# RWKV mixer steps laid on other ticks between the matmuls of a hybrid SSD and RWKV-7 block

## The chip, the cores and the metric

The kernel runs on one core of a Trainium2 chip. The metric is the device time of one execution in microseconds (us). Before the change it is 1671.96 us, the median of three runs (1670.29 to 1674.27). The engines are TensorE (PE, with its weight loads PEld), VectorE (DVE), ScalarE (ACT), GpSimd (POOL) and SyncE (SP), which issues the DMAs.

## What is computed

One block of a streaming encoder on x of 256 frames by 2048 channels: a norm, one input projection, two mixers (a Mamba-2 SSD and an RWKV-7), one output projection, and a SwiGLU FFN. The change touches the RWKV-7 mixer alone. Its core in the reference:

```
def step(S, inp):
    r_t, w_t, k_t, v_t, a_t, b_t = inp
    sa = jnp.einsum('bhvk,bhk->bhv', S, a_t)
    S = S * w_t[:, :, None, :] + sa[..., None] * b_t[:, :, None, :] + v_t[..., None] * k_t[:, :, None, :]
    return S, jnp.einsum('bhvk,bhk->bhv', S, r_t)
...
y = wkv7_scan(rh, decay.reshape(b, s, H, N), kh, vh, -kk, kk * ah)
mu = jnp.mean(y, axis=-1, keepdims=True)
var = jnp.mean(jnp.square(y - mu), axis=-1, keepdims=True)
y = ((y - mu) * lax.rsqrt(var + GN_EPS)).reshape(b, s, D_RWKV) * gn_w.astype(f32) + gn_b.astype(f32)
bonus = jnp.sum(rh * kh * r_k.astype(f32).reshape(H, N), axis=-1, keepdims=True) * vh
y = y + bonus.reshape(b, s, D_RWKV)
return y * g
```

The kernel does the scan in four chunks of 64 frames, for 32 heads, four heads (256 channels, a "pair" of channel blocks) at a time: eight pairs, 0 to 7.

## The kernel before

**Main matmuls.** Every projection is done as three fp32r matmuls (high by high, low by high, high by low). A weight unit of 512 KB is loaded by SP into `raw` (4 buffers), rounded by ACT into `whi` (L192), and the rest is subtracted by DVE into `wlo` (L193), four buffers each, so ACT and DVE can run up to four units ahead of PE. `gemm_a` (L277 to L279) takes four units of 24 matmuls for 256 columns; `gemm_b` (L305 to L307) takes units of 12 matmuls and adds its result into h (L318).

**Stretches.** The RWKV part runs over the pairs. The stretch of pair pi holds the three `gemm_a` of its k, v and r (12 units) and, from pair 4 on, behind v, two column groups of the output projection of finished pairs (4 units). So the stretches of pairs 0 to 3 are short (12 units) and those of pairs 4 to 7 long (16 units). A `gemm_a` advances a clock of ticks by four, a column group by two: 12 and 16 ticks. Two more windows follow, behind the last pair, of 20 and 18 ticks.

**Side work.** `window(pi, ticks)` lays the steps of three pairs on these ticks, in the class `Side`, a heap that is emptied as the clock passes: preparation of pair pi (table `PREP`), matrices of pair pi-1 (`AMATS`) and the inverse of its chunk matrices (`INV`), and the chain over the chunks of pair pi-2 (`CHAIN`). In short stretches, `INV` and `CHAIN` are multiplied by 11.5/16. What is not placed when a stretch ends is emitted there by `drain`. A step is a group of instructions of several engines; a scheduler then makes each engine's order out of the emitted program and the tiles' buffers. Each engine works through its order strictly.

**The steps that matter here.**

- `recept` and `sums` (L541 to L567): `sums` multiplies r by k on DVE, sums per head (`red`, L539), adds the halves on PE (`ps_sum`, L557) and makes `nn` and `bon`.
- `amat` and `across`: products of ar with bt and kt on PE (`ps_a`, L602 and L619), masked by DVE into `atb` and `atk` (L605, L622).
- `inv_out` sends the 16x16 blocks of `atb` out by eight DMAs and reads them back as rows (`nb`); `inv_rows`, `inv_level(4)` and `inv_level(8)` invert them on DVE (`pd`, L685, `tt` and `xb`, L687), doubling from 4x4 to 8x8 and to 16x16 blocks; `inv_in` takes `xb` out and back (`sc_X`, `cm`) and makes `X` on DVE (L701); `lev16a`, `lev16b`, `lev32a` and `lev32b` double on to 64 on PE (`ps_b`, L712) with DVE or ACT steps between (`t1s`, `XT`, `XF`).
- For each chunk c of 0 to 3: `step_r` (`ps_r`, L766, copied by ACT to `rs`), `step_w` (`ps_w`, L780, scaled by DVE to `ws`), `step_s` (the state `ps_s`, L796 and L799, made `sn` by DVE, L804 to L807; and the result `ps_y`, L814, copied by ACT to `Y`).
- `gnorm`: mean on DVE, eight squares on ACT (`ysq`, L833), a table load and a square root (L834), reciprocal and product on DVE, eight scalings on ACT (L838). `gnorm2` and `final` apply the weights, the bonus and the gate, and hand over yh and yl for the output projection. `vt`, `btt`, `ktt` and `yc` are transposes whose quarters ACT copies (L581).

The 8 PSUM banks stand in two pools of four: one for the main matmuls, one for all the side steps.

Of the kernel before, what the change touches and what calls it, by code (L numbers as in the profile page):

```python
# [16 lines left out]
P = 128  # L17
# [14 lines left out]


PREP = (1.081, 1.2, 4.2, 5.2, 5.536, 6.756, 8.05, 9.2)
AMATS = (0.132, 1.4, 2.027, 2.231, 2.69, 3.323, 6.493)
INV = (4.9, 5.9, 6.9, 8.4, 10.4, 11.4, 12.9, 14.9)
STEPS = (0.667, 2.0, 5.0)
SSD = (0.9, 2.7, 4.842, 6.642, 8.442, 8.924, 10.724, 12.524, 12.657, 16.124)
CHAIN = (0.05, 0.6, 1.4, 2.4, 3.4, 4.0, 4.9, 5.9, 6.5, 7.4, 8.4, 9.0, 9.9, 11.4, 12.9, 13.4)


class Side:
# [26 lines left out]
def tile_hybrid_block(ctx: ExitStack, tc: tile.TileContext, x, norm1_g, w_in, conv_w, conv_b, dt_bias, A_log, D_skip,  # L69
# [16 lines left out]
    side = Side()  # L86
# [4 lines left out]
    def mxt(name):  # L91
        return mx.tile([P, 512], F32, name=name, tag="mx")

    def bc(ap, n):
        return ap.unsqueeze(ap.ndim).broadcast_to(list(ap.shape) + [n])
# [346 lines left out]
    NCH = 8  # L442

    def rwkv_pair(pi, st):
        cb0 = 2 * pi

        def tl(name, shape=(P, 2, T), bufs=1, tag=None):
            return rp.tile(list(shape), F32, name=name, tag=tag or name, bufs=bufs)

        def pl(name, shape=(P, 2, T), bufs=1):  # L450
            return pp.tile(list(shape), F32, name=name, tag=name, bufs=bufs)

        def col(c, base, j):
            return c[:, base + cb0 + j:base + cb0 + j + 1]

        def ch(t):
            return t.rearrange("p b (c t) -> p (b c) t", c=4)
# [78 lines left out]
        def headsum(dst, src):  # L536
            tr = pl("tmp2", (P, NCH, 64))
            nc.vector.transpose(tr.rearrange("p c t -> p (c t)"), src.rearrange("p b t -> p (b t)"))
            nc.vector.tensor_reduce(dst.rearrange("p c s -> p (c s)"),  # L539
                                    tr.rearrange("p c (s t) -> p (c s) t", t=32), axis=AX.X, op=ALU.add)  # L540
# [7 lines left out]
        def sums():  # L548
            red, r, kp = st["red"], st["r"], st["kp"]
            rk = pl("tmp")  # L550
            for j in range(2):
                nc.vector.scalar_tensor_tensor(rk[:, j], r[:, j], col(colA, RK, j), kp[:, j], ALU.mult, ALU.mult)
            headsum(red[:, 1], rk)
            ps = mxt("ps_sum")
            po = ps[:, :16].rearrange("p (a c) -> p a c", a=2)
            for s in range(2):
                nc.tensor.matmul(po, sel[:, s], red[:, :, :, s], start=s == 0, stop=s == 1)  # L557

            nn = tl("nn", (P, NCH + 4), 3)
            nc.vector.tensor_scalar(nn[:, :NCH], po[:, 0], 1e-24, -2.0, ALU.max, ALU.mult)  # L560
            nc.vector.reciprocal(nn[:, :NCH], nn[:, :NCH])
            for hh in range(2):
                nc.scalar.copy(hd(nn, 1 - hh)[:, NCH:], hd(nn, hh)[:, 4:NCH])
            bon = tl("bon", (P, NCH), 3)
            nc.vector.tensor_copy(bon, po[:, 1])
            st["nn"], st["bon"] = nn, bon

        def hd(t, hh):
            return t[hh * 64:(hh + 1) * 64]
# [20 lines left out]
        def amat(name, key, half):  # L590
            def f():
                if half == 0:
                    st[name] = tl(name, (P, NCH, 2, 64), 2)
                dst = st[name]
                src = ch(st[key])
                if name == "atb" and half == 1:
                    across(dst, src)
                    return
                ps = mxt("ps_a").rearrange("p (c t) -> p c t", c=4)
                for c in range(4):  # L600
                    for hh in range(2):
                        nc.tensor.matmul(hd(ps, hh)[:, c], hd(src, hh)[:, half * 4 + c],  # L602
                                         hd(st["ar"], hh)[:, half * 4 + c].rearrange("p a t -> p (a t)"),
                                         start=True, stop=True)
                nc.vector.tensor_tensor(dst[:, half * 4:half * 4 + 4].rearrange("p c a t -> p c (a t)"), ps,  # L605
                                        mask2.rearrange("p a t -> p (a t)").unsqueeze(1).broadcast_to([P, 4, P]),
                                        ALU.mult)
                if name == "atb":
                    d = dst[:, 0:4, 0]
                    nc.vector.tensor_tensor(d, d, bc(st["nn"][:, 0:4], 64), ALU.mult)  # L610
            return f

        def across(dst, src):

            pa = [mxt("ps_a")[:, :256].rearrange("p (c t) -> p c t", c=4) for _ in range(2)]
            for c in range(4):
                for a in range(2):
                    for hh in range(2):
                        nc.tensor.matmul(hd(pa[a], hh if a else 1 - hh)[:, c], hd(src, hh)[:, 4 + c],  # L619
                                         hd(st["ar"], hh)[:, 4 + c, a], start=True, stop=True)  # L620
            for a in range(2):
                nc.vector.tensor_tensor(dst[:, 4:8, a], pa[a], mask2[:, a].unsqueeze(1).broadcast_to([P, 4, 64]),  # L622
                                        ALU.mult)
            d = dst[:, 4:8, 0]
            nc.vector.tensor_tensor(d, d, bc(st["nn"][:, NCH:NCH + 4], 64), ALU.mult)
# [148 lines left out]
        def step_w(c):  # L774
            def f():
                rs = st["rs"]
                pw = [mxt("ps_w")[:, :64] for _ in range(2)]
                for hh in range(2):
                    for j in range(2):
                        nc.tensor.matmul(hd(pw[j], 1 - hh if j else hh), hd(st["XF"], hh)[:, 4 * j + c],  # L780
                                         hd(rs, hh)[:, j], start=True, stop=True)
                ws = tl("ws", (P, 2, 64), 2)
                for j in range(2):
                    nc.vector.tensor_scalar(ws[:, j], pw[j], st["nn"][:, 4 * j + c:4 * j + c + 1], None, ALU.mult)
                st["ws"] = ws
            return f
# [37 lines left out]

        def gnorm():
            Y = st["Y"]
            mv = tl("mv", (P, 2, NCH), 2)
            nm, rs = mv[:, 0], mv[:, 1]
            nc.vector.tensor_reduce(nm, Y, axis=AX.X, op=ALU.add)
            nc.vector.tensor_scalar(nm, nm, -1.0 / 64, None, ALU.mult)  # L830
            sq = tl("ysq", (P, NCH, 64))
            for c in range(NCH):
                nc.scalar.activation(sq[:, c], Y[:, c], AF.Square, bias=nm[:, c:c + 1], accum_out=rs[:, c:c + 1])  # L833
            nc.scalar.activation(rs, rs, AF.Sqrt, bias=epsg, scale=1.0 / 64)  # L834
            nc.vector.reciprocal(rs, rs)
            nc.vector.tensor_tensor(nm, nm, rs, ALU.mult)
            for c in range(NCH):
                nc.scalar.activation(Y[:, c], Y[:, c], AF.Identity, bias=nm[:, c:c + 1], scale=rs[:, c:c + 1])  # L838

# [14 lines left out]
        def final():  # L854
# [3 lines left out]
            for j in range(2):  # L858
                for kk in range(2):
# [7 lines left out]
            nc.scalar.copy(yh, yo)  # L867
            nc.vector.tensor_tensor(yl, yo, yh.bitcast(F32), ALU.subtract)

        amats = [recept, sums, amat("atb", "bt", 0), amat("atb", "bt", 1), inv_out, amat("atk", "kt", 0),  # L870
                 amat("atk", "kt", 1)]
        inv = [inv_rows, inv_level(4), inv_level(8), inv_in, lev16a, lev16b, lev32a, lev32b]
        chain = [load2]
        for c in range(4):
            chain += [step_r(c), step_w(c), step_s(c)]
        chain += [gnorm, gnorm2, final]
        return dict(load=load, decay=decay, rate=rate, keys=keys, keys2=keys2, keysum=keysum, vt=tok("vt", "v"),
                    btt=tok("btt", "bt"), ktt=tok("ktt", "kt"), amats=amats, inv=inv, chain=chain)

    pairs = []  # L880

    def window(pi, ticks):
        if pi < 8:
            w = pairs[pi]
            w["load"]()
            for t, n in zip(PREP, ("decay", "rate", "keys", "keys2", "keysum", "btt", "vt", "ktt")):
                side.at(t, w[n])
        if 0 < pi < 9:
            w = pairs[pi - 1]
            for t, f in zip(AMATS, w["amats"]):  # L890
                side.at(t, f)
            for t, f in zip(INV, w["inv"]):
                side.at(t if ticks >= 16 else t * (ticks - 0.5) / 16, f)
        if pi > 1:
            for t, f in zip(CHAIN, pairs[pi - 2]["chain"]):
                side.at(t if ticks >= 16 else t * (ticks - 0.5) / 16, f)

    held = []

# [8 lines left out]
    for pi in range(8):  # L908
        st = {}
        pairs.append(rwkv_pair(pi, st))  # L910
        window(pi, 16 if pi > 3 else 12)
        for i, (n, c) in enumerate((("k", CK), ("v", CV), ("r", CR))):
            ps = scaled(gemm_a(w_in, [(0, 256, c + pi * 256)], "ps_rkv"))
            t = pp.tile([P, 2, T], F32, name="rkv", tag="t" + n, bufs=1)
# [139 lines left out]
    for g in range(4):  # L1054
# [5 lines left out]
        for i in range(2):  # L1060
            ps = scaled(gemm_a(w_in, [(0, 256, CXBC + g * 512 + i * 256)], "ps_xs"))
            t = xz.tile([P, 2, T], F32, name="xc", tag=f"xc{i}")
# [98 lines left out]
    for b in range(2):  # L1161
        r = finish(2, b)
        for n in (2, 3, 0, 1):
            c = slice(n * 512, (n + 1) * 512)
            t = hg[b][n]
# [33 lines left out]
```

## Time and profile before

| What | Value |
|---|---|
| median of 3 runs | 1671.96 us (1670.29 to 1674.27) |
| profiled execution | 1671.13 us, of it the span 1669.4 us |
| mean granted clock of PE | 0.996 |
| PE busy | 1640.1 us, 98% of the span |
| DVE busy | 1172.9 us, 70% |
| ACT busy | 910.7 us, 55% |
| DMA read from HBM | 281.75 MB |

The span is the profiled part of the execution; 1.7 us lie around it. "Busy" is the time in which the engine had at least one instruction under way. A wait of an engine is put down to the instruction that released it. "Granted clock" is the clock that the throttle allows PE, 1 being full. The RWKV stretches lie between 38 and 512 us, the SSD part behind them up to 930 us, the FFN from there to the end.

### The profile page before, as it was taken

How to read it: one execution, taken by the hardware profiler on the slowest of the kernel's cores; microseconds unless marked ns; L12 is line 12 of the kernel's file. 1: busy time of each engine (PE TensorE's matmuls, PEld its weight loads, DVE VectorE, ACT ScalarE, POOL GpSimd, SP SyncE). 2: the span in 40 equal slices, each digit the busy share in tenths (PEclk: the TensorE clock that was granted, in tenths of full speed). 3: DMA queues.
4: the chain of work that ended last, by engine and by line, in shares of the span. 5: the costliest groups of instructions: out<-in, count | busy, mean ns of one | idle time of the engine just before them, and what ended most of it. 6: DMA issues, size and time to landing. Idle time of an engine off the chain costs nothing.

```text
span 1669.4 us, 31147 instructions
## 1 busy us (share of the span) xinstructions
PE 1640.1 (98%) x12514; PEld 1422.7 (85%) x12514; DVE 1172.9 (70%) x1827; ACT 910.7 (55%) x1488; POOL 17.9 (1%) x57
## 2 busy tenths in 40 slices
PE   8999999999999999999999999999999999999997
PEld 8998898988888988998988888888888888888886
DVE  7887898788887867877778656465565564554657
ACT  6654775766755648657665544444444444444444
POOL 3000000000000000000000000000000000000000
PEclk9998999999999999999999999999999999999999
DMA  8653554454455556765655666666666666666663
GB/s 247 184 143 104 134 135 126 137 140 139 138 142 144 154 152 188 233 191 155 180 176 152 202 189 190 194 189 189 196 190 189 190 189 196 189 191 192 190 189 126
DMA packets 219473, 286.97 MB, mean 172 GB/s; under 512 B 41762, under 2 KB 124480, under 8 KB 218688
## 3 DMA queue, kind: packets, MB, share of 16 engines
q1 hardware_dynamic: 218000, 282.68, 58.1%
q8 instruction: 98, 1.61, 0.4%
q0 software_dynamic: 752, 1.24, 0.3%
q10 hardware_dynamic: 576, 1.05, 0.2%
q14 instruction: 47, 0.39, 0.1%
HBM read 281.75 MB, written 3.18 MB: 171 GB/s over the span
## 4 chain that ended last, share of the span: by engine, by line
PE 77%; DVE 9%; ACT 6%; issue 3%; DMA 3%; SPq 1%; DVEq 0%; POOL 0%; ACTq 0%
PE ps_o L305 8%; PE ps_o L306 8%; PE ps_o L307 8%; PE ps_gt L306 5%; PE ps_up L307 5%; PE ps_gt L305 5%; PE ps_up L306 5%; PE ps_gt L307 5%; PE ps_up L305 5%; DVE wlo L193 2%; PE ps_xs L277 2%; ACT whi L192 2%; PE ps_rkv L277 2%; PE ps_xs L278 2%; PE ps_xs L279 2%
## 5 line engine op out<-in xcount | busy, mean ns | idle before, releaser
L193 DVE TENSOR_TENSOR wlo<-raw,whi 128x1024 fp32r<-128x1024 f32 x508 | 619.9, 1222 | 376.9 <-ACT whi L192 375.8
L192 ACT CAST whi<-raw 128x1024 fp32r<-128x1024 f32 x508 | 532.7, 1051 | 596.8 <-PE ps_o L307 159.6
L277 PE MATMUL ps_rkv<-uh,whi 128*128 128x256 f32 x768 | 227.7, 296 | 0.0
L279 PE MATMUL ps_rkv<-uh,wlo 128*128 128x256 f32 x768 | 218.9, 285 | 0.0
L278 PE MATMUL ps_rkv<-ul,whi 128*128 128x256 f32 x768 | 218.8, 285 | 0.0
L277 PEld LDWEIGHTS ps_rkv<-uh,whi 128*128 128x128 f32 x768 | 147.5, 192 | 5.3 <-issue 0.7
L278 PEld LDWEIGHTS ps_rkv<-ul,whi 128*128 128x128 f32 x768 | 147.9, 193 | 1.2 <-issue 0.3
L279 PEld LDWEIGHTS ps_rkv<-uh,wlo 128*128 128x128 f32 x768 | 147.6, 192 | 0.4
L305 PE MATMUL ps_gt<-whi,uh 128*128 128x512 f32 x352 | 137.1, 389 | 0.0
L307 PE MATMUL ps_gt<-whi,ul 128*128 128x512 f32 x352 | 137.0, 389 | 0.0
L306 PE MATMUL ps_gt<-wlo,uh 128*128 128x512 f32 x352 | 136.9, 389 | 0.0
L305 PE MATMUL ps_up<-whi,uh 128*128 128x512 f32 x352 | 136.9, 389 | 0.0
L306 PE MATMUL ps_up<-wlo,uh 128*128 128x512 f32 x352 | 136.9, 389 | 0.0
L307 PE MATMUL ps_up<-whi,ul 128*128 128x512 f32 x352 | 136.9, 389 | 0.0
L305 PE MATMUL ps_o<-whi,ah 128*128 128x512 f32 x336 | 131.7, 392 | 0.0
L307 PE MATMUL ps_o<-whi,al 128*128 128x512 f32 x336 | 130.9, 390 | 0.0
L306 PE MATMUL ps_o<-wlo,ah 128*128 128x512 f32 x336 | 130.7, 389 | 0.0
L305 PE MATMUL ps_o<-whi,yh 128*128 128x512 f32 x256 | 105.6, 412 | 0.0
L307 PE MATMUL ps_o<-whi,yl 128*128 128x512 f32 x256 | 100.9, 394 | 0.0
L306 PE MATMUL ps_o<-wlo,yh 128*128 128x512 f32 x256 | 100.8, 394 | 0.0
L318 DVE TENSOR_TENSOR h<-ps_o,h 128x512 f32<-128x512 f32 x152 | 98.5, 682 | 1.7 <-PE ps_o L307 1.1
L306 PEld LDWEIGHTS ps_up<-wlo,uh 128*128 128x128 f32 x352 | 66.1, 188 | 13.7
(342 smaller groups left out, 2982.4 us busy)
## 6 DMA issues: line engine op xcount, KB each, us to landing
raw<-in_w_in_dram SPq DMA_DIRECT2D x180, 512.0 KB, 4.0
raw<-in_w_gate_dram SPq DMA_DIRECT2D x88, 512.0 KB, 3.7
raw<-in_w_up_dram SPq DMA_DIRECT2D x88, 512.0 KB, 3.7
raw<-in_w_down_dram SPq DMA_DIRECT2D x88, 512.0 KB, 4.6
raw<-in_w_out_dram SPq DMA_DIRECT2D x32, 512.0 KB, 4.0
raw<-in_w_out_dram SPq DMA_DIRECT2D x32, 256.0 KB, 4.2
raw<-in_w_out_dram SPq DMA_DIRECT2D x64, 128.0 KB, 4.0
csb<-cs_d SPq DMA_DIRECT2D x4, 1024.0 KB, 6.5
```

What stands on the lines that cost most here:

```text
L192: order(nc.scalar.copy(hi, raw))
L193: order(nc.vector.tensor_tensor(lo, raw, hi.bitcast(F32), ALU.subtract))
L277: nc.tensor.matmul(o, wh, uh[:, kt], start=first and b == 0, stop=False)
L278: nc.tensor.matmul(o, wh, ul[:, kt], start=False, stop=False)
L279: nc.tensor.matmul(o, wl, uh[:, kt], start=False, stop=last and b == 1)
L305: nc.tensor.matmul(ps[b], ah[:, s], hi[:, k], start=first, stop=False)
L306: nc.tensor.matmul(ps[b], ah[:, s], lo[:, k], start=False, stop=False)
L307: nc.tensor.matmul(ps[b], al[:, s], hi[:, k], start=False, stop=last)
L318: nc.vector.tensor_tensor(d, ps[b], d, ALU.add)
```

## The change

No instruction is added and none taken away. `sums` is split into `sums` (the products and `red`) and `norms` (`ps_sum` and what follows); `gnorm` into `gnorm` (mean and squares), `gscale` (root, reciprocal, product) and `gapply` (the eight scalings). The tables give their ticks, and the long stretches get new ones. `inv_level(8)` moves from 6.9 to 8.1, behind the state of the third chunk (`step_s(2)`, 7.4 before and 7.6 now). `inv_out` moves from 2.69 to 3.9. The short stretches get tables of their own, `INV12` and `CHAIN12`, in the place of the scaled ones.

```
 PREP = (1.081, 1.2, 4.2, 5.2, 5.536, 6.756, 8.05, 9.2)
-AMATS = (0.132, 1.4, 2.027, 2.231, 2.69, 3.323, 6.493)
-INV = (4.9, 5.9, 6.9, 8.4, 10.4, 11.4, 12.9, 14.9)
+AMATS = (0.132, 1.6, 2.9, 3.1, 3.6, 3.9, 4.6, 6.6)
+INV = (5.9, 6.4, 8.1, 9.4, 11.4, 12.4, 13.4, 15.4)
+INV12 = (5.4, 5.9, 6.4, 7.4, 9.4, 10.4, 10.9, 11.9)
...
-CHAIN = (0.05, 0.6, 1.4, 2.4, 3.4, 4.0, 4.9, 5.9, 6.5, 7.4, 8.4, 9.0, 9.9, 11.4, 12.9, 13.4)
+CHAIN = (0.05, 0.4, 1.4, 2.4, 3.4, 4.4, 5.1, 6.1, 6.9, 7.6, 8.9, 9.9, 10.4, 11.4, 12.4, 12.9, 13.4, 13.9)
+CHAIN12 = (0.05, 0.4, 1.4, 2.4, 3.4, 4.4, 4.9, 5.9, 6.9, 7.4, 8.4, 9.4, 9.9, 10.4, 10.9, 11.1, 11.4, 11.9)
...
             headsum(red[:, 1], rk)
+
+        def norms():
+            red = st["red"]
             ps = mxt("ps_sum")
...
         def gnorm():
             Y = st["Y"]
-            mv = tl("mv", (P, 2, NCH), 2)
+            st["mv"] = mv = tl("mv", (P, 2, NCH), 2)
...
+
+        def gscale():
+            nm, rs = st["mv"][:, 0], st["mv"][:, 1]
             nc.scalar.activation(rs, rs, AF.Sqrt, bias=epsg, scale=1.0 / 64)
             nc.vector.reciprocal(rs, rs)
             nc.vector.tensor_tensor(nm, nm, rs, ALU.mult)
+
+        def gapply():
+            Y, nm, rs = st["Y"], st["mv"][:, 0], st["mv"][:, 1]
             for c in range(NCH):
...
-            for t, f in zip(INV, w["inv"]):
-                side.at(t if ticks >= 16 else t * (ticks - 0.5) / 16, f)
+            for t, f in zip(INV if ticks >= 16 else INV12, w["inv"]):
+                side.at(t, f)
         if pi > 1:
-            for t, f in zip(CHAIN, pairs[pi - 2]["chain"]):
-                side.at(t if ticks >= 16 else t * (ticks - 0.5) / 16, f)
+            for t, f in zip(CHAIN if ticks >= 16 else CHAIN12, pairs[pi - 2]["chain"]):
+                side.at(t, f)
```

What this makes of the engines' orders, at three places. The line numbers in the changed kernel are 2 to 11 higher than before.

PE, in the k projection of a long stretch (here pair 6's), before: the products that become `atb` (ps_a), then state and result of chunk 0 (ps_s, ps_y). ps_sum stands 11 rows ahead of this piece.

```order
L602 MATMUL ps_a<-ar,bt 64x128 x8
L619 MATMUL ps_a<-ar,bt 64x64 x16
L796 MATMUL ps_s<-vt,ktt 64x64 x2
L799 MATMUL ps_s<-ws,btt 64x64 x2
L796 MATMUL ps_s<-vt,ktt 64x64 x2
L799 MATMUL ps_s<-ws,btt 64x64 x2
L814 MATMUL ps_y<-vt,atk 64x64 x4
L814 MATMUL ps_y<-ws,atb 64x64 x4
```

And now, behind the same number of main matmuls:

```order
L801 MATMUL ps_s<-vt,ktt 64x64 x2
L804 MATMUL ps_s<-ws,btt 64x64 x2
L801 MATMUL ps_s<-vt,ktt 64x64 x2
L804 MATMUL ps_s<-ws,btt 64x64 x2
L819 MATMUL ps_y<-vt,atk 64x64 x4
L819 MATMUL ps_y<-ws,atb 64x64 x4
L279 MATMUL ps_rkv<-uh,whi 128x256
```

State and result of chunk 0 now stand ahead of everything; ps_sum comes 12 main matmuls later, the first ps_a 24 later, the second (ps_a of `across`) 36 later.

DVE, at the end of a long stretch's v projection (here pair 7's), before: the last doubling (pd, tt, xb) around the state of the third chunk (sn) and a wlo.

```order
L685 TENSOR_TENSOR pd<-nb,xb 64x512
L193 TENSOR_TENSOR wlo<-raw,whi 128x1024
L575 STREAM_TRANSPOSE btt<-bt 128x512
L687 TENSOR_REDUCE tt<-pd 64x64
L804 TENSOR_TENSOR sn<-ps_s,sn 128x128
L685 TENSOR_TENSOR pd<-xb,tt 64x512
L805 TENSOR_TENSOR sn<-sn,pt 128x128
L687 TENSOR_REDUCE xb<-pd 64x8x8
```

And now:

```order
L690 TENSOR_TENSOR pd<-nb,xb 64x512
L233 TENSOR_TENSOR ps_rkv<-ps_rkv,R 128x512
L580 STREAM_TRANSPOSE btt<-bt 128x512
L809 TENSOR_TENSOR sn<-ps_s,sn 128x128
L363 SCALAR_TENSOR_TENSOR rkv<-ps_rkv,colA,rkv 128x255
L810 TENSOR_TENSOR sn<-sn,pt 128x128
L692 TENSOR_REDUCE tt<-pd 64x64
L580 STREAM_TRANSPOSE ktt<-kt 128x512
L363 SCALAR_TENSOR_TENSOR rkv<-ps_rkv,colA,rkv 128x255
L690 TENSOR_TENSOR pd<-xb,tt 64x512
L579 STREAM_TRANSPOSE tmp_7246<-rkv 128x512
L692 TENSOR_REDUCE xb<-pd 64x8x8
```

The wlo stands ahead of this piece now, with six other instructions between, and the end of v's projection (ps_rkv, rkv) and two transposes have come into it. `X` stands behind the third wlo after it, and behind the second before.

ACT, where the short stretches give way to the long ones (pair 4's k and v), before: between two casts of weights (whi).

```order
L192 CAST whi<-raw 128x1024
L770 COPY rs<-ps_r 128x64 x2
L360 ACTIVATE rkv<-ps_rkv,omA 128x256
L487 ACT_TABLE_LOAD
L487 ACTIVATE th<-ps_lw,hwa 128x256 x2
L507 ACTIVATE ta<-ps_la,hwa 128x256
L488 ACTIVATE th<-th,half 128x512
L507 ACTIVATE ta<-ps_la,hwa 128x256
L516 ACTIVATE kp<-ta,oka,hwa 128x256
```

And now, from the same weight unit's cast on:

```order
L194 CAST whi<-raw 128x1024
L838 ACTIVATE ysq,mv<-Y,mv 128x64 x8
L744 COPY t1s<-ps_b 32x256 x2
L842 ACT_TABLE_LOAD
L842 ACTIVATE mv<-mv,epsg 128x8
L586 COPY vt<-tmp_3292 32x8x32 x4
L849 ACTIVATE Y<-Y,mv 128x64 x3
L586 COPY ktt<-tmp_3343 32x8x32 x4
L849 ACTIVATE Y<-Y,mv 128x64 x5
L861 COPY vx<-ysq 64x256 x2
L756 COPY XF<-ps_b 32x8x32 x2
L775 COPY rs<-ps_r 128x64 x2
```

The norm of pair 1 (squares, root, scalings), which lay some four weight units earlier, now stands behind this cast; the piece shown above for before follows behind the next cast, together with the copies of `yc`.

More of the change, by code (lines that the diff above doesn't have):

```diff
@@ L868, in final @@
             nc.vector.tensor_tensor(yl, yo, yh.bitcast(F32), ALU.subtract)
-        amats = [recept, sums, amat("atb", "bt", 0), amat("atb", "bt", 1), inv_out, amat("atk", "kt", 0),
+        amats = [recept, sums, norms, amat("atb", "bt", 0), amat("atb", "bt", 1), inv_out, amat("atk", "kt", 0),
                  amat("atk", "kt", 1)]
@@ L875, in rwkv_pair @@
             chain += [step_r(c), step_w(c), step_s(c)]
-        chain += [gnorm, gnorm2, final]
+        chain += [gnorm, gscale, gapply, gnorm2, final]
         return dict(load=load, decay=decay, rate=rate, keys=keys, keys2=keys2, keysum=keysum, vt=tok("vt", "v"),
```

## The prediction

> **What bounds the kernel now.** First the page: its span and the busy shares.
>
> ```profile
> span 1669.4 us, 31147 instructions
> ...
> PE 1640.1 (98%) x12514; PEld 1422.7 (85%) x12514; DVE 1172.9 (70%) x1827; ACT 910.7 (55%) x1488; POOL 17.9 (1%) x57
> ...
> PEclk9998999999999999999999999999999999999999
> ```
>
> TensorE (PE) is busy for 98% of the span. The last row is its granted clock in forty slices, in tenths: full but for the slice at 125 us. The change adds no matmul and takes none away, so it can only work on the 29.3 us in which PE stands, and on its clock. Second, the waits of PE:
>
> ```profile
> PE ps_b L712 <- DVE X L701: 2.9, 2, 2.2
> PE ps_r L766 <- DVE sn L805: 2.2, 5, 0.7
> PE ps_R L225 <- DVE rstd L214: 2.1, 1, 2.1
> PE ps_w L780 <- ACT rs L770: 2.0, 3, 0.8
> PE ps_y L814 <- DVE atb L622: 1.9, 4, 0.5
> PE ps_n L247 <- DMA h<-in_x_dram: 1.8, 1, 1.8
> PE ps_sum L557 <- DVE red L539: 1.6, 4, 0.5
> ```
>
> The columns are us in total, times, longest. ps_R and ps_n belong to the opening norm. The other five are waits of RWKV mixer steps, 10.6 us together. That is most of what there is and nearly all that re-laid steps can give back. Third, the same view for 293 to 500 us, which holds the heads of the long stretches of pairs 5 to 7 and parts of their neighbours:
>
> ```profile
> PE ps_y L814 <- DVE atb L622: 1.4, 3, 0.5
> PE ps_sum L557 <- DVE red L539: 1.4, 3, 0.5
> PE ps_r L766 <- DVE sn L805: 1.3, 3, 0.7
> ```
>
> The long stretches repeat the same three stops, about 1.4 us a stretch. The X wait (2.9) and the rs wait (2.0) are not in this part: they belong to the short stretches. Fourth, the windows view, with the busy time of PE, PEld, DVE, ACT and POOL, then the granted clock:
>
> ```profile
> 125.00:135.50 10.50, 9.41 (x183) 8.73 (x183) 6.88 (x12) 1.04 (x1) 0.12 (x1) 0.52 0.47 137
> ...
> 428.00:495.00 67.00, 65.56 (x854) 58.74 (x853) 57.82 (x112) 45.07 (x104) 0.56 (x3) 1.00 0.49 139
> ```
>
> The last row is one whole period of the long stretches: VectorE (DVE) works for 57.8 of 67 us, so a step laid later on DVE quickly becomes late for PE. The first row is a second loss: from 125 to 135.5 us the clock stood at 0.52.
>
> **The change part by part.** The sum is made against the profiled execution, 1671.13 us (1669.4 of span and 1.7 around it). That is 0.8 us under the median of 1671.96, inside the three runs' 1670.29 to 1674.27.
>
> *Heads of the long stretches.* ps_sum stands today right behind the vector work on red, and y of the first chunk stands behind two blocks of ps_a whose results (atb) hold PSUM. In the new order y stands ahead of both, and ps_sum, now a step of its own, comes about half a unit after it. With 1.4 + 1.4 = 2.8 us in three stretches removed, I take **−2.8**. Nothing else is queued for PE there but main matmuls whose weights are ready. The bounds are 0 (the wait reappears at the ps_a blocks, now a unit later) and −3.5 (the totals of the two rows over the whole program).
>
> *Doubling of 8x8 blocks behind the third state.* The doubling ends with xb, which goes out and back by DMA and returns as X; X starts the 16-blocks on PE. Today, in pair 7's stretch, on DVE:
>
> ```profile
> 481.62 0.70 DVE L687 TENSOR_REDUCE xb<-pd 64x64 f32<-64x512 f32 x1
> ...
> 486.84 0.43 DVE L701 TENSOR_TENSOR X<-cm,pmask 128x256 f32<-128x256 f32 x1
> ```
>
> and the user on PE:
>
> ```profile
> 488.96 1.11 PE L712 MATMUL ps_b<-X,atb 32*32 32x32 f32 x64
> ```
>
> X is done at 487.27, so it has 1.7 us to spare. From xb to X it is 4.5 us, by way of two DMAs on SP, where the change moves the pair's eight atb transfers and the two of X past a few weight loads, without adding one. In the new order 17 instructions stand on DVE between a wlo and the doubling's last reduction, and 5 today; some six of the 17 only changed sides of that wlo, and about ten are new ahead of it. At the 0.4 to 0.7 us of the two rows, X comes 5 to 7 us later. PE's block comes one unit later too, with a few steps moved ahead of it: some 4 to 5 us, an estimate from the 67 us of a period with its 16 units, 4.2 us each. So X would come between 1.7 us early and 1.3 us late; the nearest row is today's 1.7 to spare, which the later doubling about uses up. The r3 wait on sn (2.2 over five stretches) goes the same way: sn waits behind longer DVE work, but r3 also stands later. If PE waits at r3 it doesn't wait at X. I take **+1.0** for both over all long stretches, bounds −2.2 (r3's whole wait gone) and +5 (1.3 us in four stretches).
>
> *Own table for the short stretches.* Today the short stretches use the long table, scaled by 11.5/16, so the norm of the pair two back ends at about four fifths of it. With the new table it ends in the last tick. ScalarE (ACT) then has that whole tail at the border to the next stretch. The same work today, at a border where it lies spread with the casts (whi) between:
>
> ```profile
> 229.74 1.28 ACT L834 ACT_TABLE_LOAD   x1
> 231.03 0.30 ACT L834 ACTIVATE mv<-mv,epsg 128x8 f32<-128x8 f32 x1
> 231.36 0.82 ACT L850 COPY vx<-ysq 64x256 f32<-64x256 f32 x2
> 232.20 1.05 ACT L192 CAST whi<-raw 128x1024 fp32r<-128x1024 f32 x1
> 233.28 1.65 ACT L581 COPY vt<-tmp 32x256 f32<-32x256 f32 x4
> 234.95 2.76 ACT L838 ACTIVATE Y<-Y,mv 128x64 f32<-128x64 f32 x8
> 237.74 1.65 ACT L581 COPY ktt<-tmp 32x256 f32<-32x256 f32 x4
> 239.41 0.75 ACT L739 COPY t1s<-ps_b 32x256 f32<-32x256 f32 x2
> ...
> 245.66 1.04 ACT L192 CAST whi<-raw 128x1024 fp32r<-128x1024 f32 x1
> ...
> 254.70 1.03 ACT L192 CAST whi<-raw 128x1024 fp32r<-128x1024 f32 x1
> ...
> 257.78 1.05 ACT L192 CAST whi<-raw 128x1024 fp32r<-128x1024 f32 x1 [1.17 <-PE ps_rkv L278]
> ...
> 274.24 1.05 ACT L192 CAST whi<-raw 128x1024 fp32r<-128x1024 f32 x1 [3.51 <-PE ps_rkv L278]
> ```
>
> and the squares, from the groups of 176 to 243 us:
>
> ```profile
> L833 ACT ACTIVATE ysq<-Y,mv 128x64 f32<-128x64 f32 x8 | 2.7, 339 | 0.0
> ```
>
> In the new order, at the border from pair 3 to pair 4, all this lies between two casts: whi 1.05, squares 2.7, t1s 0.75, table 1.28, root 0.3, vt 1.65, Y 2.76, ktt 1.65, vx 0.82 = 13.0 us. Between that cast and the next lies today's block of 245.66 to 254.70 (9.0 us, of it 1.1 idle), and the copies of yc as well (as long as vt, 1.65): 9.6 to 10.7. So the third cast starts some 23 us after the first. The casts at 257.78 and 274.24 lie four units apart, 16.5 us, and wait for PE's matmuls: PE takes 4.1 us a unit here, and lets ACT run four units ahead. The first cast can start when PE has freed its buffer, and PE wants the third five units later, 20.6 us. It gets it at 23 + 1.05 + a subtraction on DVE, about 25. By that PE waits 4.5 us; the units there hold more mixer work than the average, which takes off up to as much again. Queued behind the long ACT block are the casts; behind them the subtractions, and PE. I take 2.0, a little under the middle, and the same a stretch earlier, where the squares come as late: **+4.0**, bounds 0 and +9.
>
> What the new table takes away are the waits at short distances, since it leaves 1.0 tick between a chunk's r and w, where 0.6 × 11.5 / 16 = 0.43 stood: rs 2.0. X at 125 us stays as late, since its DMAs and its DVE work move with it: 0, bounds −2.9 and +3. So **−2.0**.
>
> *The clock.* In this trace the half clock begins just when PE has waited 2.2 us for X; 10.5 us at 0.52 cost up to 10.5 × 0.48 = 5.0 us, of which I take 4 as an estimate, because the small matmuls there are not bound by the clock alone. As the wait for X stays, I leave this at **0**: one such dip before and one after. [...]
>
> *Table loads.* Gscale's split adds no load. [...]
>
> **Sum:** −2.8 + 1.0 + 4.0 − 2.0 + 0 = +0.2. 1671.13 + 0.2 = **1671.3 us**.
>
> **The rivals.**
>
> *Faster (0.34).* The scheduler lays the ACT blocks where PE has enough units ahead, so the +4.0 is 0 or 1, and X at 125 us comes early enough that the clock does not dip (−4). For it: the units at the border hold more work than average. Against: the order shows two casts and 23 us of ACT work. Then −2.8 + 1 + 0.5 − 2.0 = −3.3 and with the dip's gain −7.3: 1664 to 1668.
>
> *Slower (0.30).* One mechanism: at the two borders the bunched ACT work starves PE of whi for over about 2.2 us, the length that sufficed at 125 us, and the clock halves there. Price: 4.5 instead of 2.0 us at a border and 4 us of half clock, so 6.5 more for one border and 13 for both: 1678 to 1684, the first the likelier, since not every wait of that length dipped.
>
> *The change does nothing in the long stretches.* Ps_sum and atb only hand their wait to the next user, and X eats the rest: 1674 by the sum without −2.8. That lies in the no-change case (0.36) with the forecast itself.
>
> **How the numbers follow.** A measurement of this kernel can tell about 0.2%, 3.3 us, from no change. Forecast (no change) 0.36, faster 0.34, slower 0.30. The range 1663 to 1680 takes in the faster case whole and one dipped border, and leaves out both. The forecast's own range is 1668 to 1675, since cases of both signs hold most of the chance.
>
> **What would show it.** Right at the long heads: no rows ps_sum on red and ps_y on atb after 300 us. Right on X: waits at ps_b on X at each long stretch, under 1 us, and r3 on sn no larger. Right at the borders: whi or wlo as the releaser of ps_rkv near 190 and 245 us, with 13 us between casts. Wrong: a clock row at 0.5 elsewhere than at 125 us or none at all, or r3 and X waits of 2 us in each long stretch, which would make it slower without any border.

## The result, and the profile after

The changed kernel takes 1685.2 us (median of 4 runs, 1683.31 to 1686.84), beside 1672.28 us for the kernel before in the same runs: a ratio of 1.0076, with a 95% interval of 1.0062 to 1.0089. It is slower by 0.8%, 12.9 us. The forecast was no change, 1671.3 us, within 1663 to 1680. The time lies outside this range; the rival that priced two starved borders stood at 1684.

The page of the changed kernel, the lines that answer to those shown of before:

```profile
span 1683.0 us, 31139 instructions
...
PE 1650.2 (98%) x12514; PEld 1428.3 (85%) x12514; DVE 1176.2 (70%) x1827; ACT 912.4 (54%) x1488; POOL 18.1 (1%) x57
...
PEclk9999999999999999999999999999999999999999
```

The span grew by 13.6 us, with the same work on each engine. PE stands 32.8 us instead of 29.3, and is "busy" 10 us longer; a matmul in flight counts as busy, also while the clock is halved (from 423.5 to 426.5 us PE is busy throughout at a granted clock of 0.50) or the next one is held up for less than its own length (0.28 us for a main matmul). So the page alone does not say where the time went. PE's waits do, in part (us in total, times, longest; line numbers are 2 to 11 higher than before):

```profile
PE ps_b L717 <- DVE X L706: 4.3, 3, 2.4
PE ps_s L804 <- DVE ws L789: 2.9, 2, 1.7
PE ps_rkv L281 <- DVE wlo L195: 2.0, 1, 2.0
PE ps_R L227 <- DVE rstd L216: 2.0, 1, 2.0
PE ps_y L819 <- DVE tt L692: 1.9, 1, 1.9
PE ps_b L717 <- DVE mv L835: 1.7, 2, 1.2
PE ps_n L249 <- DMA h<-in_x_dram: 1.5, 1, 1.5
PE ps_lw L487 <- ACT XF L756: 1.2, 2, 0.7
PE ps_up L118 <- DVE eps L107: 1.1, 1, 1.1
PE ps_b L717 <- DVE X L711: 1.1, 2, 0.9
PE ps_rkv L279 <- ACT whi L194: 0.9, 1, 0.9
PE ps_o L308 <- DVE wlo L195: 0.8, 1, 0.8
```

The rows of before for rs, sn and y on atb are gone, and red is down from 1.6 to 0.2. New among the mixer's rows are ws, wlo, whi, tt, mv and XF. Outside the opening norm, the largest single ones after X (2.4) are the main matmuls' wait for wlo (2.0) and y's for tt (1.9).

The clock fell elsewhere, and more often. In the windows view of the changed kernel the granted clock is the number ahead of the last two:

```profile
25.00:35.00 10.00, 8.05 (x53) 7.79 (x54) 7.26 (x19) 4.78 (x10) 1.64 (x3) 0.83 0.83 205
155.00:170.00 15.00, 13.12 (x152) 12.36 (x151) 11.99 (x31) 6.30 (x13) 0.23 (x1) 0.89 0.16 43
195.00:215.00 20.00, 17.01 (x237) 15.28 (x237) 16.93 (x37) 16.09 (x34) 0.12 (x1) 0.91 0.37 98
230.00:255.00 25.00, 23.32 (x348) 21.53 (x349) 18.91 (x31) 11.45 (x30) 0.56 (x3) 0.86 0.48 127
415.00:430.00 15.00, 13.29 (x132) 11.02 (x131) 13.34 (x32) 6.25 (x13) 0.00 (x0) 0.89 0.37 107
```

In rows of 0.5 us the granted clock of these stretches reads 0.50 or 1.00, but for the rows in which it turns. So a mean of 0.89 over 15 us is 3.3 us at half clock and the rest at full. Worked out so, the five rows hold 3.4 + 3.3 + 3.6 + 7.0 + 3.3 = some 20 us at half clock, against 10 us before. That is worth at most 5 us of the difference, of which 1.7 us fall in the opening norm (first row), which the change leaves alone.

Where the time lies is seen best by stretch. The end of a stretch is read from the timeline, as the start of the DVE multiplication that follows r's last matmul. Lengths in us; the column "2 to 4" is the sum of the three, and steps that move over a border cancel in it:

| Kernel | pair 2 | pair 3 | pair 4 | 2 to 4 | 5 to 7 |
|---|---|---|---|---|---|
| before | 66.1 | 56.3 | 67.7 | 190.1 | 201.6 |
| after | 62.1 | 57.3 | 81.3 | 200.7 | 204.2 |

Of the 13.6 us, 10.6 lie in the stretches of pairs 2 to 4, that is in the two short stretches with a chain and in the one behind them, and 2.6 in the long ones of pairs 5 to 7. Behind 705 us the two kernels run 13.5 us apart to the end. The windows view of these stretches, pairs 2 to 4 and then 5 to 7, first before and then after:

```profile
119.96:310.06 190.10, 181.93 (x2645) 165.34 (x2644) 161.13 (x322) 125.82 (x302) 2.11 (x11) 0.97 0.48 127
310.06:511.66 201.60, 196.51 (x2554) 175.78 (x2553) 172.65 (x331) 135.02 (x307) 1.68 (x9) 1.00 0.50 139
```

```profile
119.44:320.14 200.70, 188.33 (x2654) 169.90 (x2654) 162.44 (x322) 125.10 (x299) 2.05 (x11) 0.97 0.44 119
320.14:524.29 204.15, 199.30 (x2566) 177.24 (x2566) 176.21 (x334) 137.42 (x310) 1.68 (x9) 0.99 0.47 132
```

In pairs 2 to 4 PE stands 12.4 us instead of 8.2, so 4.2 of the 10.6 us are waits; the other 6.4 us are time counted as busy. In pairs 5 to 7 PE stands no longer than before (4.9 us instead of 5.1): the whole 2.6 us are counted as busy.

### The profile page after: what moved, and what is told of

It reads as the page before. It is cut to its first block, busy times and chain, and to the rows that moved or that the text cites. A ratio compares the mean times of both kernels' runs of the same rounds, so it can differ in the third digit from the quotient of the medians.

```text
span 1683.0 us, 31139 instructions
## 1 busy us (share of the span) xinstructions
PE 1650.2 (98%) x12514; PEld 1428.3 (85%) x12514; DVE 1176.2 (70%) x1827; ACT 912.4 (54%) x1488; POOL 18.1 (1%) x57
## 4 chain that ended last, share of the span: by engine, by line
PE 76%; DVE 9%; ACT 7%; DMA 5%; issue 2%; SPq 1%; DVEq 0%; ACTq 0%
PE ps_o L307 7%; PE ps_o L309 7%; PE ps_o L308 7%; PE ps_gt L309 5%; PE ps_up L307 5%; PE ps_gt L307 5%; PE ps_gt L308 5%; PE ps_up L308 5%; PE ps_up L309 5%; DVE wlo L195 2%; PE ps_rkv L279 2%; PE ps_rkv L280 2%; PE ps_rkv L281 2%; PE ps_xs L279 2%; PE ps_xs L280 2%; PE ps_xs L281 2%
## 5 line engine op out<-in xcount | busy, mean ns | idle before, releaser
L309 PEld LDWEIGHTS ps_up<-whi,ul 128*128 128x128 f32 x352 | 66.1, 188 | 13.8
```

Source lines behind the costliest of these rows:

```text
L309: nc.tensor.matmul(ps[b], al[:, s], hi[:, k], start=False, stop=last)
```

## The experiments

Theory S says that the short stretches' own tables cost: they push the tail of the steps over the border, ACT's norm above all. Theory L, the rival, says that the long tables cost, with the doubling behind the third state. All experiments start from the changed source. Where all tables in force are old, the traces show the order of the kernel before: e10_new_from5 up to pair 4 on PE, DVE and ACT, e2_short_new from the middle of pair 5's stretch on DVE and ACT.

**Which table.** The short stretches alone back to the old tables:

```
+AMATS12 = (0.132, 1.4, 1.4, 2.027, 2.231, 2.69, 3.323, 6.493)
-INV12 = (5.4, 5.9, 6.4, 7.4, 9.4, 10.4, 10.9, 11.9)
+INV12 = tuple(t * 11.5 / 16 for t in <old INV>)
...
+CHAIN12 = tuple(t * 11.5 / 16 for t in <old CHAIN>)
```

> Long stretches as in the changed kernel, short stretches (pairs 0 to 3) with all three old tables, scaled as before. Theory S (the short stretches' own tables push a tail of steps over the next border; about 10 of the 13 us lie in the stretches of pairs 2 to 4): 1670 to 1675 us, and the stretch of pair 4 back to about 68 us from 81. Theory L (the doubling behind the third state makes DVE late in every long stretch): 1680 to 1685 us, since only the long tables matter.

Measured: ratio 1.0019 (0.9998 to 1.0041), 1673.9 us; the stretch of pair 4 takes 69.1 us, 5 to 7 take 199.7. The opposite, short stretches new and long ones old:

> Long stretches with the old tables, short stretches with the new ones (own tables for inverse and chain, and the new ticks of the matrices). Theory S: 1680 to 1684 us, 8 to 12 above the kernel before. Theory L: 1671 to 1674 us, as before.

Measured: ratio 1.0050 (1.0035 to 1.0065), 1679.3 us, just under the 1680 expected and 8.9 us above the kernel before in the same runs; pairs 2 to 4 take 200.4 us, as in the changed kernel, and 5 to 7 take 201.2, as before. Theory S holds. The long tables have a part, but a small and unsteady one (below).

**Inside the short tables.** The inverse's own table alone, with the old chain:

> Of the new tables only the one for the inverse in short stretches; matrices, chain and long stretches as before. If the late inverse (X waits of 1.8 us at the border to pair 4, and its blocks on PE behind the border) is what costs: 1675 to 1680 us, with the stretch of pair 4 at 75 us or more. If the late norm on ACT costs: 1670 to 1673 us.

Measured: ratio 1.0057 (1.0039 to 1.0076), 1681.0 us. The loss is as large, but not where it was expected: the stretch of pair 4 takes 68.9 us, that of pair 3 61.1 (X 2.0 and rs 1.9 us late) and that of pair 5 73.8 (ps_sum late by 3.3 us, then half clock: 0.51 from 325 to 330 us, 0.80 to 335). The chain's own table alone:

> Of the new tables only the one for the chain in short stretches; matrices, inverse and long stretches as before. If the late norm on ACT costs (casts missing at the two borders): 1676 to 1680 us, with waits of the main matmuls for whi or wlo near 200 us and a half clock there. If the late inverse costs: 1670 to 1673 us.

Measured: ratio 1.0118 (1.0080 to 1.0157), 1695.3 us, worse than everything together; pairs 2 to 4 take 212.4 us. Part of that is the clock: the four runs lie between 1683.6 us, with a mean granted clock of 0.992, and 1696.5, with 0.983. Each table alone fits the other's old place badly, so these two do not divide the loss. They only show that no half of it is harmless.

**The norm on ACT.** The squares and scalings of pairs 0 and 1, whose norms lie at the two borders (to pair 3 and to pair 4), are left out:

```
+            if pi < 2:
+                nc.vector.memset(rs, 64.0)
+                return
             for c in range(NCH):
                 nc.scalar.activation(sq[:, c], Y[:, c], AF.Square, ...
...
+            if pi < 2:
+                return
             for c in range(NCH):
                 nc.scalar.activation(Y[:, c], Y[:, c], AF.Identity, ...
```

> The changed kernel without the squares and the eight scalings of the norm of pairs 0 and 1, whose norms lie at the two borders of short stretches; that part of the computation is left out. It frees ACT of about 5.4 us at each border. If ACT starves PE there: the main matmuls' waits for whi and wlo at 202 to 205 us go, 3 to 6 us under the changed kernel, so 1679 to 1682 us. If the waits there come from DVE or from X: 1684 to 1686 us.

Measured: ratio 1.0010 (0.9995 to 1.0025), 1672.8 us. Of the 12.9 us, about 11 went, more than the 3 to 6 expected. The same left out of the kernel before is the control:

> The kernel before without the squares and the eight scalings of the norm of pairs 0 and 1, the control to e9_norm01_out; that part is left out. If these 5.4 us of ACT at each border cost PE time only where the changed kernel has laid them: 1670 to 1672 us, as before. If they cost the kernel before as much: 1660 to 1663 us, and the 12 us of e9_norm01_out say nothing of the change.

Measured: ratio 0.9993 (0.9979 to 1.0007), 1668.8 us, no difference. So leaving this work out gains nothing that can be told where the kernel before has it, and nearly all of the loss where the change has laid it.

The same test with the whole computation: the eight scalings of these two pairs on DVE.

```
+            if pi < 2:
+                for c in range(NCH):
+                    nc.vector.tensor_scalar(Y[:, c], Y[:, c], rs[:, c:c + 1], nm[:, c:c + 1], ALU.mult, ALU.add)
+                return
```

> The changed kernel with the eight scalings of pairs 0 and 1 on DVE instead of ACT, 2.8 us less on ACT at each border and 2.2 us more on DVE. If ACT alone is late there: 4 to 8 us under the changed kernel, 1677 to 1681 us, the waits for whi and wlo at 202 to 205 us gone. If ACT and DVE are both late, so that the work has no room on either: 1683 to 1688 us.

Measured: ratio 1.0000 (0.9984 to 1.0016), 1670.2 us. Moving sixteen short instructions from ACT to DVE takes back the whole loss. These edits change more than ACT's load, though: behind the first moved instruction the scheduler lays other steps otherwise too. At the first border ps_lw stands 23 main matmuls earlier on PE than in the changed kernel, and ps_sum 8 later. What ACT's time is worth alone, with all else in place, was not run. This is how ACT looks at the first border in the changed kernel (start, us, engine, line):

```profile
173.82 1.05 ACT L194 CAST whi<-raw 128x1024 fp32r<-128x1024 f32 x1 [1.83 <-PE ps_rkv L280]
178.16 0.33 ACT L825 COPY Y<-ps_y 128x64 f32<-128x64 f32 x2 [3.29 <-PE ps_y L819]
179.93 0.35 ACT L838 ACTIVATE ysq<-Y,mv 128x64 f32<-128x64 f32 x1 [1.45 <-DVE mv L835]
...
193.56 1.07 ACT L194 CAST whi<-raw 128x1024 fp32r<-128x1024 f32 x1
...
200.88 1.08 ACT L194 CAST whi<-raw 128x1024 fp32r<-128x1024 f32 x1
...
204.22 2.01 ACT L194 CAST whi<-raw 128x1024 fp32r<-128x1024 f32 x2
```

and PE behind it:

```profile
202.01 0.39 PE L279 MATMUL ps_rkv<-uh,whi 128*128 128x256 f32 x1 [0.88 <-ACT whi L194]
202.24 0.28 PE L280 MATMUL ps_rkv<-ul,whi 128*128 128x256 f32 x1
204.55 0.39 PE L281 MATMUL ps_rkv<-uh,wlo 128*128 128x256 f32 x1 [2.04 <-DVE wlo L195]
```

Between two casts, 173.82 and 193.56, it is 19.7 us: ACT first stands 4.7 us for the last result and its mean, and from the first square to the next cast it is 13.6 us. To the cast after that it is 7.3 us more. PE has used up its lead by then: it waits 0.88 us for whi and, two matmuls later, 2.04 for the wlo made from it. The half clock follows at once: from 204.8 to 204.9 us the granted clock reads 0.54, and 0.50 behind it, up to 208 us (in the row of 195 to 215 us above). With the scalings on DVE, the same rows of ACT:

```profile
177.92 0.35 ACT L838 ACTIVATE ysq<-Y,mv 128x64 f32<-128x64 f32 x1 [1.45 <-DVE mv L835]
...
188.61 1.07 ACT L194 CAST whi<-raw 128x1024 fp32r<-128x1024 f32 x1
...
195.92 1.09 ACT L194 CAST whi<-raw 128x1024 fp32r<-128x1024 f32 x1
```

10.7 us instead of 13.6, and no wait of PE for whi or wlo at this border; pair 3's stretch takes 51.8 us instead of 57.3, and pairs 2 to 4 take 190.7 instead of 200.7. PE's part of it:

```profile
119.58:310.34 190.76, 183.16 (x2653) 165.97 (x2653) 165.29 (x339) 120.05 (x285) 2.04 (x11) 0.98 0.44 123
```

PE stands 7.6 us there, 4.8 less than in the changed kernel. The other 5.1 us are time counted as busy; up to 3.5 of them can be the clock, which is at half for some 7 us in place of 14.

**Which border.** Only pair 0's scalings on DVE, so only the first border relieved (the edit above with `pi == 0`):

> As e12_scale_dve, but only pair 0's scalings go to DVE, so that only the first of the two borders (pair 2 to pair 3) is relieved. If both borders pay for the late norm: half of the way, 1676 to 1679 us. If only the first one does, where the trace of the changed kernel shows PE waiting for whi and wlo: 1669 to 1673 us, as e12_scale_dve. If only the second does: 1683 to 1686 us.

Measured: ratio 1.0023 (1.0005 to 1.0041), 1678.6 us beside 1673.8 for the kernel before on that chip. By ratios, 0.53% of the 0.76% went with the first border. The 0.23% that are left would be the second's; their interval (0.05 to 0.41%) lies above the kernel before, but overlaps that of e12_scale_dve. So that the first border pays is shown, and the second's share is not clear of the noise. Pair 3 is at 51.8 us as with both relieved, pair 4 still at 81.4 instead of 79.0, and in that stretch PE now waits for a wlo, 1.9 us at 295.56:

```profile
PE ps_rkv L281 <- DVE wlo L195: 2.1, 2, 1.9
```

The last piece, short tables new, long ones old, with the scalings of both pairs on DVE:

> As e2_short_new (short stretches new, long ones old), with the scalings of pairs 0 and 1 on DVE. If ACT's late norm is all that the short tables cost: 1668 to 1671 us, 8 to 11 under e2_short_new and not above the kernel before. If the short tables have another cost that the new long tables hide: 1674 to 1679 us.

Measured: ratio 1.0008 (0.9995 to 1.0020), against 1.0050 without the relief. In us it stands in the upper range expected (1675.4), but on a chip where the kernel before takes 1673.8, so by the ratio the first theory holds: the late norm is all of the short tables' cost that these runs can tell. Up to 0.2% more is not excluded, and in its one profile, from that same chip, pairs 2 to 4 take 196.0 us, with 10 us at half clock.

**The rows of the inverse.** In the changed kernel DVE also stands at 157 us, for the rows that come back by DMA, and PE stands behind it. DVE, then PE:

```profile
157.44 0.17 DVE L653 COPY xb<-nb 64x12 f32<-64x12 f32 x1 [3.04 <-DMA nb<-sc_n]
```

```profile
160.54 0.44 PE L819 MATMUL ps_y<-vt,atk 64*64 64x64 f32 x2 [1.88 <-DVE tt L692]
```

The short stretches' matrices and transfers got their old ticks (`AMATS12` with inv_out at 2.69):

> The changed kernel with the old ticks, in short stretches, of the sums, of atb and of the eight transfers of inv_out. If DVE's wait for the rows of the inverse (3.0 us on the DMA at 157 us, with PE behind it for 1.9 us) is a cause of its own: that wait goes, and 2 to 5 us with it, 1680 to 1683 us. If not: 1684 to 1686 us.

Measured: ratio 1.0072 (1.0053 to 1.0092), 1682.4 us. In us that lies in the range expected of a cause, but the kernel before takes 1669.7 on that chip, so the loss is the same 0.7%. PE's wait for tt is gone, the time is not: pair 2's stretch is shorter by 2.8 us, pair 3's longer by 6.7. ACT's blocks stay and PE reaches them earlier: it waits 3.6 us for whi and 3.2 for wlo, once each at either border. It is a wait that another one replaces.

**The long stretches.** The doubling of the 8x8 blocks ahead of the third state again, short stretches old:

> As e1_short_old, but in the long stretches the doubling of the 8x8 blocks goes back ahead of the third chunk's state, to 6.9. Theory L: 3 to 6 us under e1_short_old, because the waits of ps_s on ws and of ps_b on mv and X in the stretches of pairs 5 to 7 go. Theory S alone: within 1 us of e1_short_old.

Measured: ratio 1.0012 (1.0000 to 1.0023), so no difference to e1_short_old that its interval can tell. The waits on ws are not gone but grew (0.5, 0.5, 1.0 and 1.6 us in the stretches of pairs 4 to 7). Theory L falls here too. The heads alone:

> The kernel before with the split of the sums and the new ticks of the matrices in the long stretches only; inverse and chain as before. If the heads' waits (ps_sum on red, ps_y on atb, 2.8 us) can be had by these steps alone: 1669 to 1670 us, 2.5 to 3 under the kernel before. If the wait only passes to the next user: 1672 us.

Measured: ratio 1.0022 (1.0009 to 1.0036), not faster; y of the first chunk now waits for ws, 1.1 to 1.4 us a stretch. The wait passed to the next user. New tables only from pair 5 on:

> New tables only from the stretch of pair 5 on, old ones up to pair 4. If the new long tables gain where nothing is left over from short stretches: 1667 to 1670 us, 1.5 to 3 under the kernel before. If their new waits (ps_s on ws, ps_b on mv) eat the gain: 1670 to 1673 us.

Measured: ratio 1.0011 (0.9999 to 1.0023), no gain.

No version beats both kernels: the best with the whole computation, e12_scale_dve, is level with the kernel before.

## Why the prediction was wrong

**Own table for the short stretches: the mechanism was right at the first border, the price too small.** The prediction saw that ACT has the whole tail at the borders, with three casts 23 us apart, and took 2.0 us a border from a range of 0 to 4.5. The three casts are 27.1 us apart at the first border (173.82 to 200.88) and 26.2 at the second, for which the 23 were worked out (14.4 instead of 13.0, then 11.8 instead of 9.6 to 10.7). PE's waits at the first border are 0.88 + 2.04 = 2.9 us. But relieving both borders took 0.76%, 13 us by ratios, of it 0.53%, 9 us, with the first alone. So +4.0 should have been about +13, beyond its own bound of +9. The step that failed is the choice of a value for a border by the length of PE's wait for its weights alone, with the clock put at 0. What the runs show besides that wait:

- The half clock. The step "one such dip before and one after" failed: the granted clock fell five times while matmuls ran, among them at the first border and near the second. Over all the trace it is some 20 us at half clock against 10, so up to 5 us. The runs without a profile agree: their mean granted clock is 0.990 to 0.992, that of the kernel before mostly 0.994 to 0.997 on the four chips of the experiments. That not every wait of some 2 us dips held in the trace of before, where the opening norm waits 1.84 us at 8.88 us and 2.11 us at 26.84 us and the clock reads 1.00 from 0 to 40 us; with a wait of 2.00 us there, at 26.95 us, the changed kernel dips (0.50 from 27.5 to 30.5 us).
- At the second border PE waits in this trace not for casts but for X, whose cm lands late. DVE, PE and ACT there:

```profile
241.41 0.43 DVE L706 TENSOR_TENSOR X<-cm,pmask 128x256 f32<-128x256 f32 x1 [1.93 <-DMA cm<-sc_X]
```

```profile
241.98 1.50 PE L717 MATMUL ps_b<-X,atb 32*32 32x32 f32 x64 [1.68 <-DVE X L706]
```

```profile
246.69 0.33 ACT L825 COPY Y<-ps_y 128x64 f32<-128x64 f32 x2 [6.56 <-PE ps_y L819]
246.90 0.49 ACT L362 ACTIVATE rkv<-ps_rkv,omA 128x256 f32<-128x256 f32 x1
249.28 1.05 ACT L194 CAST whi<-raw 128x1024 fp32r<-128x1024 f32 x1 [1.88 <-issue]
...
263.65 1.05 ACT L194 CAST whi<-raw 128x1024 fp32r<-128x1024 f32 x1
...
275.48 1.05 ACT L194 CAST whi<-raw 128x1024 fp32r<-128x1024 f32 x1
```

X stands ahead of the fourth chunk's result on PE, and the copy of that result ahead of the next cast on ACT: ACT idles 6.6 us just ahead of its longest block, which then ends at 263.65 with the next cast, 14.4 us after 249.28. The wait for X is not what the relief took away, though: in e12_scale_dve, level with the kernel before, PE waits 1.47 us for X at the same border, with some 7 us at half clock behind it (0.86 over 230 to 255 us). What the second border's block costs is therefore not settled.

- Some 4 to 5 of the 10.6 us are in no row of waits and are more than the clock can explain (6.4 us counted as busy, less at most 2 us for 4 us more at half clock). A main matmul counts as busy for 0.28 us where the next can start 0.12 us after it (so the starts at 418.75, 418.87 and 418.99 us), so shorter pauses don't show. What each of them waits for was not settled.

The −2.0 for rs came true (the row is gone), but tt and XF (1.9 and 1.2 us) took its place: a step laid late leaves one wait and meets another. X near 130 us stayed as late as said (2.4 us).

**The heads (−2.8): the waits went, the time stayed.** After 300 us ps_sum waits 0.2 us and y on atb not at all, as said. But a wait that the prediction didn't have took their place: ws, behind the inverse's rows on DVE, 1.71, 0.33 and 1.14 us. With X, on PE:

```profile
490.10 0.33 PE L804 MATMUL ps_s<-ws,btt 64*64 64x64 f32 x4 [1.14 <-DVE ws L789]
...
504.15 1.11 PE L717 MATMUL ps_b<-X,atb 32*32 32x32 f32 x64 [1.18 <-DVE mv L835]
```

So PE stands as long as before there. The 2.6 us that pairs 5 to 7 take more (204.2 instead of 201.6) are counted as busy, and up to 1.7 of them are the half clock from 423.2 us on (0.89 over 415 to 430 us), which begins 1.5 us behind the longest wait for ws (1.71 us, to 421.72). In e1_short_old, e9_norm01_out, e15_pair0_dve, e12_scale_dve and e13_invout_early, where these stretches have the changed kernel's order, the clock stays full in them (1.00 in each row of 5 us from 310 to 510), and they take 199.7, 200.1, 201.3, 201.8 and 202.5 us. So −2.8 was, by these profiles, between −1.9 and +0.9 without a dip and +2.6 with one, X's term included.

**X behind the third state (+1.0): about right.** DVE in pair 7's stretch:

```profile
496.75 0.64 DVE L692 TENSOR_REDUCE xb<-pd 64x64 f32<-64x512 f32 x1
...
503.58 0.42 DVE L706 TENSOR_TENSOR X<-cm,pmask 128x256 f32<-128x256 f32 x1 [0.62 <-DMA cm<-sc_X]
```

From xb to X it is 6.2 us instead of 4.5, and X is 1.2 us late for PE (the row at 504.15, put down to mv, which DVE does right behind X); the forecast was between 1.7 early and 1.3 late. r's wait on sn is gone, while PE's waits for X and mv from 300 to 510 us come to 2.6, so the two together are near the +1.0.

**The rivals.** The slower one named the right mechanism, both borders and a price (1684) within 1.2 us of the median. That the price fits so well is in part luck: it took 4.5 us of waiting and 4 us of clock at each border, while the trace has 2.9 us and at most 1.7 at the first, and no wait for casts at the second. It got 0.30, and of its two prices the smaller was called the likelier. Against it stood only that not every such wait dips, which is no argument for a small price when the path meets four such chances.

## What to carry to other kernels

Work on an engine that feeds the bound one is priced not by its busy share but by the longest stretch between two of its deliveries, set against the lead that the buffers allow; here ACT was 54% busy, and 2.8 us in each of two such stretches, with the order that the scheduler made around them, made 0.8% of the kernel. Behind waits of 1.2 to 2.7 us on TensorE these traces show 0 to 20 us of half clock, and where a change makes several waits, charging the same number of dips as before is wrong. To test such a cause, move a few instructions to another engine at the one place, and compare the orders of the other engines as well, since a scheduler may change them with it: sixteen scalings told more here than the tables taken apart.

## What the runs showed of the hardware

The half clock came out differently even for the same instructions, from 0 to 20 us of it in five profiles. The kernels before, e1_short_old, e5_long_inv8_early, e6_long_heads and e10_new_from5 have the same order on PE, DVE and ACT up to pair 4, and by the timeline each waits at the same place: for X near 125 us (2.25, 1.23, 1.37, 1.39 and 2.66 us), and in all but the last once more near 130 us, ahead of the matmul with XT (0.61, 2.57, 1.92 and 2.68 us, which the trace puts down to issue). In the order named, from 120 to 150 us:

```profile
120.00:150.00 30.00, 26.11 (x453) 23.36 (x455) 18.52 (x37) 12.57 (x29) 0.56 (x3) 0.83 0.47 126
```

```profile
120.00:150.00 30.00, 26.21 (x389) 23.41 (x387) 16.09 (x32) 11.69 (x27) 0.56 (x3) 0.66 0.41 116
```

```profile
120.00:150.00 30.00, 25.65 (x460) 23.11 (x461) 20.17 (x39) 13.99 (x32) 0.56 (x3) 0.94 0.49 137
```

```profile
120.00:150.00 30.00, 24.86 (x477) 22.16 (x475) 20.69 (x41) 13.84 (x32) 0.56 (x3) 1.00 0.45 126
```

```profile
120.00:150.00 30.00, 26.27 (x469) 23.67 (x467) 20.01 (x39) 14.01 (x32) 0.56 (x3) 0.89 0.50 136
```

Means of 0.83, 0.66, 0.94, 1.00 and 0.89 over 30 us are 10, 20, 4, 0 and 7 us at half clock. Pair 2's stretch takes 66.1, 70.6, 64.3, 63.9 and 64.8 us with it. The changed kernel waits 2.4 us for X there and does not dip at all (1.00 from 120 to 150 us). No single wait there is over 2.7 us. The clock fell in four of the five profiles; in e6_long_heads, with waits of 1.39 and 2.68 us, it did not. This spread, up to 7 us in one stretch, goes on into the times. The ten runs of e1_short_old have a mean granted clock that falls from 0.997 in the fastest (1667.1 us) to 0.987 in the slowest (1684.2), nearly in the order of their times. The 0.010 between these two is about 17 us of a run of 1675, and their times are 17.0 us apart.
